# Four-chunk modulation tiles, a merged score product and alternating row halves in the first mixer of a diffusion backbone step

## The chip, the cores and the metric

The kernel runs on one core of one Trainium2 chip. The metric is the device time of one execution in microseconds. Before the change the median of three timed executions is 2934.5 us (2930.41 to 2939.74). One more execution was profiled; its own time is 2926.64 us and its span, from the first to the last instruction of the program, is 2924.9 us. All rows below come from that execution.

## The reference

One inference step for 128 context tokens and 1024 latent tokens, width 1024, in float32, through two layers. Each layer has a mixer and a SwiGLU channel mixer; both sit behind an RMSNorm that is shifted, scaled and gated by six vectors of a conditioning map. The change touches the conditioning map and the mixer of layer 0:

```python
sh1, sc1, g1, sh2, sc2, g2 = split(silu(c) @ w_ada[l] + b_ada[l], 6)      # for context and latent condition, both layers
h = rmsnorm(x, norm_mix) * (1 + sc1) + sh1
qa, ka, va, qb, kb, vb, rb, lr = split_cols(h @ w_in, SIZES_EVEN)
oa = windowed_attention(rope(qa), rope(ka), va, cached context keys, per-head sink)
# gated linear attention, per direction, in chunks of 64 tokens:
q_e, k_e, k_s = q*exp(bcum), k*exp(-bcum), k*exp(b_last - bcum)
o = where(mask, q_e @ k_e.T, 0) @ v + q_e @ S        # S: scanned state, S <- decay*S + k_s.T @ v
ob = rms(o_forward + flip(o_backward)) * gain * silu(rb)
x = x + g1 * (concat(oa, ob) @ w_out)
```

On the diagonal of a chunk the two decays cancel, so the forward and the backward score of a token with itself are both its plain q.k.

## The kernel before

Activations are kept transposed: 128 features on the partitions, 1152 tokens (128 context, 1024 latent) along the free dimension, in three chunks of 384 (`NCH`). Most products are made of three float32r matmuls over high and low parts (`mm3`, L147 to L149). The other matmuls are float32, and the profile shows two instructions for each of them. SBUF is handed out by hand as 34 slots (`us(i)`), two wider ones (`uc(0)`, `uc(1)`, shown as tile `c`), and small rings: `raw` (3 buffers of 128x1024, where weights land), `w` (4), `t` (5 of 128x384) and `ta` (3). PSUM has the rings `mm` (3 banks), `S` (2), `X` (2) and `O` (1).

The order of the instructions on each engine is set by the tile framework: it plans the program in a simulated time line (`schedule_with_timeline_sim`) and sorts independent work by that. Each engine then runs its list in order. Nearly all DMAs are issued by SyncE (SP), also in order, so a DMA that waits for its buffer holds back those behind it.

The stages of layer 0's mixer, in program order:

- Head. Four modulation units for the shift and scale of the first norm, the sum of squares of x, the first norm (`norm_k`, L268 to L274).
- Token-major and gate projections, `gla_pre`, then the projections of keys, values and queries. The change does not touch these.
- Nine turns of `attention(i - 1)`, each but the last followed by one projection (`proj`, L147 to L149) whose result is spilled to DRAM: i = 0 to 3 the queries and keys of the linear attention (`ev_spill`), i = 4 to 7 its gate `rb` with a SiLU (`ev_silu`, L984). An attention block computes scores per head (L771, L779), adds the mask and takes the maximum (L786), forms the negative bias (L789), the exponential with its sum (L791), transposes the probabilities (L803) and multiplies by the values (L814 to L816).
- Linear attention, four heads, in a software pipeline: `gla_a` (decays on DVE and ACT, products on POOL, L870, L880, L882; transposes L887; chunk states L902 with 64 contraction rows per direction, evicted by L913 on ACT and DVE), `gla_b` (four scans, L927 and L928, on DVE), `gla_c` (scores L947 with 64 contraction rows per direction, masked into two SBUF halves by a predicated copy L949, products with v L955 forward and L956 backward, product with the state L959), `gla_d` (RMS norm over the head, gain, and the product with the gate read back from DRAM, L975). Between them `out_a` multiplies the attention output with a quarter of the output projection.

A modulation unit (`ada_unit`) before covers 512 of the 6144 outputs of a layer. Its weights come as four DMAs of 512 KB (L188), each holding two contraction chunks of 128 for 512 columns. Each contraction chunk is one matmul (L192) with a stationary of 32 columns that writes a group of 32 PSUM partitions, group k % 4. ACT copies the 512 columns out (L195, twice 256), matmuls with a selector add the four groups (L198), DVE adds the bias (L203) and for scales the norm weight (L207). Four units run in the head, with slots of their own; twenty in the loop, through two buffers (`uc(0)`, `uc(1)`): two per turn at i = 5 to 8, then three after each `gla_c`.

Of the kernel before, what the change touches and what calls it, by code (L numbers as in the profile page):

```python
# [14 lines left out]
D = 1024  # L15
# [31 lines left out]
def body(tc, A):  # L47
# [6 lines left out]
    with contextlib.ExitStack() as ctx:  # L54
# [17 lines left out]
        mq = st.tile([128, 2, 128], U8, name="mq")  # L72
        dls = st.tile([128, 36], F32, name="dls")
# [106 lines left out]
        def ada_unit(l, u, raws=None, tag="mm"):  # L180
# [3 lines left out]
            for p in range(4):  # L184
                raw = raws[p] if raws else uc(aring[0] % 2)
                aring[0] += 1
                raw = raw[:, :D]
# [6 lines left out]
            for i in range(2):  # L194
                sc.copy(th[i], ps[:, i * 256:(i + 1) * 256])  # L195
            ps2 = ps[:, 0:8]
            for c in range(4):
                pe.matmul(ps2[:, 2 * c:2 * c + 2], th[c // 2][:, c % 2 * 128:(c % 2 + 1) * 128], sel[:, 0:2],  # L198
                          start=True, stop=True)
            j, k0 = u // 2, (u % 2) * 4  # L200
            m = mods[:, (l * 6 + j) * 16:(l * 6 + j + 1) * 16].rearrange("p (c k) -> p c k", c=2)[:, :, k0:k0 + 4]
            b = C_BADA + l * 48 + j * 8 + k0
            ve.tensor_tensor(out=m, in0=ps2.rearrange("p (k c) -> p c k", c=2),  # L203
                             in1=cols[:, None, b:b + 4].to_broadcast([128, 2, 4]), op=ALU.add)
            if j in (1, 4):
                n0 = (C_NMIX if j == 1 else C_NFFN) + l * 8 + k0
                ve.scalar_tensor_tensor(m, m, 1.0, cols[:, None, n0:n0 + 4].to_broadcast([128, 2, 4]),  # L207
                                        op0=ALU.add, op1=ALU.mult)
# [3 lines left out]
        def ada_all():  # L212
            for l in range(2):
                for u in range(12):
                    if l or u >= 4:
                        yield ada_unit(l, u)
# [355 lines left out]
        for u, s0 in ((0, 8), (2, 12)):  # L572
            ada_unit(0, u, [us(s0 + p) for p in range(4)], "X")
        rs = rstd_of(X, 0)
        etm_land(0)
        for u, ss in ((1, (4, 5, 6, 7)), (3, (28, 29, 30, 31))):
            ada_unit(0, u, [us(i) for i in ss], "X")
# [149 lines left out]
        def attention(b):  # L727
# [29 lines left out]
            for g in range(2):  # L757
# [3 lines left out]
                P = [PU[i // 2][:, (i % 2) * 512:(i % 2) * 512 + w] for i in range(4)]  # L761
                for i in range(4):
# [22 lines left out]
                    else:  # L785
# [3 lines left out]
                    ve.scalar_tensor_tensor(negm[:, i:i + 1], mx[:, i:i + 1], -0.125, nsink[:, h:h + 1],  # L789
                                            op0=ALU.mult, op1=ALU.min)  # L790
                    sc.activation(out=P[i], in_=src, func=AF.Exp, scale=0.125, bias=negm[:, i:i + 1],  # L791
                                  accum_out=ssum[:, i:i + 1])
# [32 lines left out]
        def ev_spill(dst, by):  # L825
            def ev(c, ps):
                t = tmp()
                if c != 1:
# [12 lines left out]
        def gla_init():  # L841
            mqf = tmpa(256)
            sy.dma_start(out=mqf, in_=A["gmask"])
            ve.tensor_copy(mq.rearrange("p a b -> p (a b)"), mqf)
# [4 lines left out]
        def gla_a(hd):  # L849
# [47 lines left out]
            for hf in range(2):  # L897
                p = slice(hf * 64, hf * 64 + 64)
                for b0, b1 in GRP:
                    ps = aux()  # L900
                    for b in range(b0, b1):
                        pe.matmul(ps[:, (b - b0) * 128:(b - b0 + 1) * 128], ktt[p, b * 128:(b + 1) * 128],  # L902
                                  vb3[p, b], start=True, stop=True)
                    pv = ps[:, :(b1 - b0) * 128].rearrange("p (b v) -> p b v", b=b1 - b0)
# [26 lines left out]
        def gla_c(hd):  # L931
# [6 lines left out]
            for b0, b1 in ((0, 4), (4, 8), (8, 9)):  # L938
                nb = b1 - b0
                t = G["AT"][atr[0] % 2]  # L940
                atr[0] += 1
                af, ab = t[:, 0:512], t[:, 512:1024]
                for q, at in ((0, af), (1, ab)):
                    ps = aux("X", 2)
                    p = slice(q * 64, q * 64 + 64)
                    for b in range(b0, b1):
                        pe.matmul(ps[:, (b - b0) * 128:(b - b0 + 1) * 128], kt[p, b * 128:(b + 1) * 128],  # L947
                                  qt[p, b * 128:(b + 1) * 128], start=True, stop=True)
                    ve.copy_predicated(at[:, :nb * 128].rearrange("p (b i) -> p b i", b=nb),  # L949
                                       mq[:, q:q + 1].to_broadcast([128, nb, 128]),  # L950
                                       ps[:, :nb * 128].rearrange("p (b i) -> p b i", b=nb))
# [28 lines left out]

        def ev_silu(dst):
            def ev(c, ps):
# [7 lines left out]
        for i in range(9):  # L990
# [3 lines left out]
            if i >= 5:  # L994
                ada_step(2)
# [417 lines left out]
```

## Time and profile before

| | |
|---|---|
| median of three timed executions | 2934.5 us |
| the profiled execution, its own time | 2926.64 us |
| its span | 2924.9 us |
| PE busy | 2747.6 us (94%) |
| DVE, ACT, POOL busy | 2096.2, 1318.0, 1299.6 us |
| mean granted TensorE clock | 0.962 of full speed |

A granted clock of 1.0 is TensorE's upper level of 2.4 GHz and 0.5 its lower one of 1.2 GHz; a mean in between is a stretch that held both. "Busy" for PE counts a matmul from its start to its modelled end, so that overlapping matmuls count once. An idle time is put down to the instruction that ended it. SP is the queue that issues DMAs. From 850 us on the kernel is the channel mixer of layer 0 and all of layer 1, whose code the diff leaves alone.

### The profile page before, as it was taken

What the parts mean: (1) busy time and instruction counts of PE and PEld (TensorE: products, weight loads), DVE (VectorE), ACT (ScalarE), POOL (GpSimd) and SP (SyncE); (2) the same over time, 40 slices, a digit from 0 to 9 for tenths busy, and PEclk for the clock granted to TensorE, in tenths of its full rate; (3) what the DMA queues carried; (4) which work ended last, traced back from release to release, by engine and by line L of the source; (5) the groups of instructions that cost most, each with busy time, mean ns of one, the idle gap of its engine ahead of it and who ended that gap; (6) DMA issues with size and microseconds to landing.
All of it is one profiled execution on the core that took longest, in us unless ns stands there. A gap on an engine that the chain in (4) does not pass through costs nothing. (4 is left out here: it accounts for less than half of the span.)

```text
span 2924.9 us, 47943 instructions
## 1 busy us (share of the span) xinstructions
PE 2747.6 (94%) x18456; PEld 2593.8 (89%) x18456; DVE 2096.2 (72%) x3589; ACT 1318.0 (45%) x2268; POOL 1299.6 (44%) x760
## 2 busy tenths in 40 slices
PE   6999989989999999999999999887899999999998
PEld 4889766766889999999999899787899999999998
DVE  5475667554388878777778787767688878778876
ACT  4344776322353433433534466544443444344333
POOL 4231013220365645555556533343555556355553
PEclk9999998799999999999999999999899999999999
DMA  7123357545253322632323223463253232533332
GB/s 274 57 82 100 105 157 231 152 143 166 72 212 95 98 87 82 214 102 85 92 89 105 72 83 114 130 212 130 100 184 93 89 94 86 188 91 114 95 89 69
DMA packets 138548, 353.55 MB, mean 121 GB/s; under 512 B 14768, under 2 KB 64304, under 8 KB 138320
## 3 DMA queue, kind: packets, MB, share of 16 engines
q1 hardware_dynamic: 136592, 343.42, 36.8%
q0 software_dynamic: 1728, 7.08, 0.7%
q8 instruction: 145, 2.38, 0.3%
q14 instruction: 83, 0.68, 0.1%
HBM read 286.14 MB, written 64.30 MB: 120 GB/s over the span
## 5 line engine op out<-in xcount | busy, mean ns | idle before, releaser
L147 PE MATMUL mm<-u,w 128*128 128x384 f32 (+1 forms) x1229 | 397.1, 324 | 10.7 <-DVE u L313 9.9
L148 PE MATMUL mm<-u,w 128*128 128x384 f32 (+1 forms) x1229 | 393.3, 320 | 3.8 <-POOL u L144 2.9
L149 PE MATMUL mm<-u,w 128*128 128x384 f32 (+1 forms) x1236 | 395.0, 320 | 0.0
L139 POOL TENSOR_TENSOR w<-raw,w 128x1024 fp32r<-128x1024 f32 (+2 forms) x67 | 148.3, 2214 | 384.1 <-ACT w L138 326.6
L147 PEld LDWEIGHTS mm<-u,w 128*128 128x128 f32 x1229 | 234.8, 191 | 30.8 <-issue 25.1
L149 PEld LDWEIGHTS mm<-u,w 128*128 128x128 f32 x1236 | 235.9, 191 | 8.1 <-issue 7.8
L148 PEld LDWEIGHTS mm<-u,w 128*128 128x128 f32 x1229 | 235.0, 191 | 5.7 <-POOL u L144 3.2
L149 PE MATMUL mm<-u,u 128*128 128x288 f32 x693 | 204.3, 297 | 0.4 <-POOL u L441 0.4
L147 PE MATMUL S<-u,w 128*128 128x288 f32 (+1 forms) x526 | 163.1, 311 | 39.9 <-ACT u L1158 17.8
L313 DVE SCALAR_TENSOR_TENSOR u<-mm,mods,u 128x288 f32<-128x288 f32 (+4 forms) x345 | 145.3, 452 | 69.7 <-PE mm L149 66.2
L147 PE MATMUL mm<-u,u 128*128 128x288 f32 x627 | 186.6, 298 | 3.7 <-ACT u L440 3.7
L148 PE MATMUL mm<-u,u 128*128 128x288 f32 x627 | 185.7, 296 | 0.0
L147 PE MATMUL X<-u,w 128*128 128x288 f32 (+1 forms) x571 | 174.3, 307 | 7.5 <-DVE u L144 2.4
L148 PE MATMUL X<-u,w 128*128 128x288 f32 (+1 forms) x571 | 175.1, 307 | 1.7 <-DVE u L274 1.7
L149 PE MATMUL X<-u,w 128*128 128x288 f32 (+1 forms) x573 | 175.0, 306 | 1.8 <-POOL w L139 1.2
L148 PE MATMUL S<-u,w 128*128 128x288 f32 (+1 forms) x526 | 161.5, 307 | 0.2 <-DVE u L144 0.2
L147 PE MATMUL mm<-u,c 128*128 128x288 f32 (+1 forms) x495 | 152.3, 308 | 2.4 <-DVE u L313 1.7
L149 PE MATMUL S<-u,w 128*128 128x288 f32 (+1 forms) x502 | 153.3, 305 | 0.0
L148 PE MATMUL mm<-u,c 128*128 128x288 f32 (+1 forms) x495 | 151.3, 306 | 0.0
L447 POOL TENSOR_TENSOR u<-raw 128x512 f32<-128x512 f32 x82 | 135.9, 1658 | 29.3 <-DMA raw<-in_w_fi_dram 13.7
L443 DVE TENSOR_TENSOR u<-u,raw 128x512 f32<-128x512 f32 x82 | 142.8, 1741 | 0.8
L147 PE MATMUL X<-u,u 128*128 128x288 f32 (+1 forms) x444 | 133.1, 300 | 7.0 <-DVE u L313 4.6
(430 smaller groups left out, 9327.6 us busy)
## 6 DMA issues: line engine op xcount, KB each, us to landing
raw<-in_w_fi_dram SPq DMA_DIRECT2D x164, 512.0 KB, 3.6
c<-in_w_ada_dram SPq DMA_DIRECT2D x80, 512.0 KB, 3.8
raw<-in_w_fo_dram SPq DMA_DIRECT2D x96, 384.0 KB, 3.1
d_w<-u SPq DMA_DIRECT2D x20, 512.0 KB, 3.4
u<-d_w SPq DMA_DIRECT2D x20, 512.0 KB, 5.4
u<-in_w_ada_dram SPq DMA_DIRECT2D x16, 512.0 KB, 10.3
raw<-in_w_fo_dram SPq DMA_DIRECT2D x16, 512.0 KB, 3.8
raw<-in_w_oi_dram SPq DMA_DIRECT2D x16, 512.0 KB, 4.0
```

Source lines behind the costliest of these rows:

```text
L139: gp.tensor_tensor(out=lo[:, :n], in0=raw[:, :n], in1=f_(hi[:, :n]), op=ALU.subtract)
L147: pe.matmul(ps, wh, hh, start=first, stop=False)
L148: pe.matmul(ps, wh, hl, start=False, stop=False)
L149: pe.matmul(ps, wl, hh, start=False, stop=last)
L313: ve.scalar_tensor_tensor(x, ps[:, s0:s1], mod(l, j, cond, n), x, op0=ALU.mult, op1=ALU.add)
L443: ve.tensor_tensor(out=s2, in0=s1, in1=a11, op=ALU.subtract)
L447: gp.tensor_tensor(out=s3, in0=a11, in1=a21, op=ALU.subtract)
```

## The change

- A modulation unit covers 256 outputs. One DMA of 512 KB now holds four contraction chunks for 256 columns, so that four matmuls for four different groups of 32 PSUM partitions follow each other. There are 24 units per layer with two DMAs each.
- The weights of the units in the loop land in five places in turn: the three buffers of the ring `raw`, which the weights of the projections use too, and `uc(0)` and `uc(1)`.
- Units are spread anew: two in each of the nine turns of the attention loop, six after each of the first three `gla_c`, the last four after the fourth. The head makes the same columns in the order shift, scale, shift, scale in steps of 256.
- In attention the bias is formed for two heads at once, after the scores of both, and then their two exponentials follow.
- The SiLU of the gate moves from the projection's eviction (now a plain DVE copy) to `gla_d`, where all three chunks are loaded first, into the ring `t`, then passed through the SiLU.
- In `gla_a` and `gla_c` the matmuls of the two row halves alternate, into two PSUM banks that are evicted afterwards.
- In `gla_c` both directions' scores are copied into one tile (the backward mask now leaves out the diagonal), POOL multiplies it by one plus the identity (`m2`), and one product with v replaces two.

```diff
@@ ada_unit
-            for p in range(4):
-                raw = raws[p] if raws else uc(aring[0] % 2)
+            for p in range(2):
+                if raws:
+                    raw = raws[p]
+                else:
+                    aring[0] = (aring[0] + 1) % 5
+                    raw = uc(aring[0] - 3) if aring[0] > 2 else pw.tile([128, D], F32, name="raw", bufs=3)
                 sy.dma_start(out=raw, in_=A["w_ada"][l, u, p])
-                for i in range(2):
-                    k = 2 * p + i
-                    g = k % 4
-                    pe.matmul(ps[32 * g:32 * g + 32, :], scp[:, k], raw[:, i * 512:(i + 1) * 512], start=k < 4, stop=k >= 4)
-            th = [tmp(256), tmp(256)]
+                for g in range(4):
+                    pe.matmul(ps[32 * g:32 * g + 32, :256], scp[:, 4 * p + g], raw[:, g * 256:(g + 1) * 256],
+                              start=p == 0, stop=p == 1)
+            th = tmp(256)
@@ attention
-                    ve.scalar_tensor_tensor(negm[:, i:i + 1], mx[:, i:i + 1], -0.125, nsink[:, h:h + 1],
+                    srcs.append(src)
+                    if i % 2 == 0:
+                        continue
+                    ve.scalar_tensor_tensor(negm[:, i - 1:i + 1], mx[:, i - 1:i + 1], -0.125, nsink[:, h - 1:h + 1],
                                             op0=ALU.mult, op1=ALU.min)
-                    sc.activation(out=P[i], in_=src, func=AF.Exp, scale=0.125, bias=negm[:, i:i + 1],
+                    for n in (i - 1, i):
+                        sc.activation(out=P[n], in_=srcs[n], func=AF.Exp, ...
@@ gla_a (the same alternation in gla_c)
-            for hf in range(2):
-                p = slice(hf * 64, hf * 64 + 64)
-                for b0, b1 in GRP:
-                    ps = aux()
-                    for b in range(b0, b1):
-                        pe.matmul(ps[:, (b - b0) * 128:(b - b0 + 1) * 128], ktt[p, b * 128:(b + 1) * 128],
+            for b0, b1 in GRP:
+                pp = [aux(), aux()]
+                for b in range(b0, b1):
+                    for hf in range(2):
+                        p = slice(hf * 64, hf * 64 + 64)
+                        pe.matmul(pp[hf][:, (b - b0) * 128:(b - b0 + 1) * 128], ktt[p, b * 128:(b + 1) * 128],
@@ gla_c
+                for q in range(2):
+                    ve.copy_predicated(at3, mq[:, q:q + 1].to_broadcast([128, nb, 128]), ...
+                gp.tensor_tensor(out=at3, in0=at3, in1=m2[:, None, :].to_broadcast([128, nb, 128]), op=ALU.mult)
-                    pe.matmul(po[:, o:o + 128], vb3[:, b], af[:, o:o + 128], start=True, stop=False)
-                    pe.matmul(po[:, o:o + 128], vb3[:, b], ab[:, o:o + 128], start=False, stop=False)
+                    pe.matmul(po[:, o:o + 128], vb3[:, b], at[:, o:o + 128], start=True, stop=False)
@@ gla_d
+            rts = [tmp() for c in range(NCH)]
+            for c in range(NCH):
+                sy.dma_start(out=rts[c], in_=d_r[hd][:, ch(c)])
+            for c in range(NCH):
+                sc.activation(out=rts[c], in_=rts[c], func=AF.Silu)
...
-                rt = tmpa()
-                sy.dma_start(out=rt, in_=d_r[hd][:, ch(c)])
-                ve.tensor_tensor(out=sd, in0=sd, in1=rt, op=ALU.mult)
+                ve.tensor_tensor(out=sd, in0=sd, in1=rts[c], op=ALU.mult)
@@ the loops
-            if i >= 5:
-                ada_step(2)
+            ada_step(2)
...
-        ada_step(3)
+        ada_step(6)
```

## Rows read from the trace of the kernel before

**Rows 1.** The page's first parts: busy time; granted clock in 40 slices.

```profile
PE 2747.6 (94%) x18456; PEld 2593.8 (89%) x18456; DVE 2096.2 (72%) x3589; ACT 1318.0 (45%) x2268; POOL 1299.6 (44%) x760
PEclk9999998799999999999999999999899999999999
```

**Rows 2.** Windows: length; PE, PEld, DVE, ACT, POOL busy (count); clock, DMA, GB/s.

```profile
0.00:50.00 50.00, 26.82 (x132) 12.98 (x133) 22.67 (x46) 21.00 (x47) 15.95 (x17) 0.90 0.89 327
230.00:425.00 195.00, 185.80 (x1111) 159.63 (x1109) 114.16 (x325) 129.59 (x267) 19.20 (x11) 0.98 0.36 111
425.00:490.00 65.00, 55.24 (x283) 36.84 (x285) 47.62 (x126) 44.77 (x102) 18.72 (x13) 0.89 0.77 222
490.00:757.00 267.00, 246.27 (x1329) 185.26 (x1326) 129.06 (x183) 80.84 (x148) 56.49 (x41) 0.85 0.52 160
516.00:552.00 36.00, 35.61 (x159) 28.37 (x159) 24.42 (x34) 13.50 (x28) 10.38 (x13) 0.51 0.51 146
604.00:624.00 20.00, 11.96 (x44) 6.47 (x43) 15.32 (x8) 3.38 (x4) 8.33 (x2) 0.66 0.35 116
725.00:757.00 32.00, 28.30 (x142) 19.09 (x142) 6.48 (x17) 4.71 (x11) 1.09 (x2) 0.89 0.51 166
```

**Rows 3.** Windows of line 192 alone, in the head.

```profile
18.43:19.50 1.07, 1.06 (x8) 0.16 (x8) 1.00 1.02 406
23.55:24.62 1.07, 1.05 (x4) 0.14 (x4) 1.00 1.06 421
```

**Rows 4.** Windows of line 192 alone: attention, then linear attention.

```profile
230.00:490.00 260.00, 29.86 (x122) 4.20 (x124) 0.96 0.46 139
490.00:757.00 267.00, 58.55 (x200) 7.20 (x196) 0.85 0.52 160
```

**Rows 5.** Waits, 490:757 on PE, 225:760 on SP: total, times, longest.

```profile
PE O L959 <- DVE u L928: 10.6, 2, 6.6
PE mm L192 <- DMA c<-in_w_ada_dram: 7.0, 5, 2.3
...
SPq L188 <- PE mm L192: 154.6, 62, 10.1
```

**Rows 6.** Windows of PE alone, mixed row halves, then one row half.

```profile
596.04:597.46 1.42, 1.42 (x19) 1.00 0.99 387
599.08:600.17 1.09, 1.09 (x9) 1.00 1.38 327
```

**Rows 7.** Lines 947 and 956: ns min/median/max, first and last start.

```profile
L947 PE MATMUL X<-u,u x144: 272/272/580, 491.3 to 671.4; 64*128 64x128 f32 x144
L956 PE MATMUL O<-u,u x72: 272/275/580, 502.7 to 717.7; 128*128 128x128 f32 x72
```

**Rows 8.** Line 913, the evictions of the chunk states.

```profile
L913 ACT COPY u<-S x20: 387/1108/1115, 484.5 to 668.8; 64x512 f32<-64x512 f32 x12, 64x128 f32<-64x128 f32 x4, 64x384 f32<-64x384 f32 x4
```

**Rows 9.** A POOL product (line 447), then scans beside POOL (timeline).

```profile
L447 POOL TENSOR_TENSOR u<-raw x82: 1277/1632/1826, 832.7 to 2849.4; 128x512 f32<-128x512 f32 x82
...
604.63 4.78 POOL L880 TENSOR_TENSOR u<-u,u 128x1152 f32<-128x1152 f32 x1 [5.05 <-DMA u<-d_qk]
607.00 4.82 DVE L928 TENSOR_TENSOR_SCAN u<-u,u 64x1152 f32<-64x1152 f32 x1
616.65 2.55 DVE L928 TENSOR_TENSOR_SCAN u<-u,u 64x1152 f32<-64x1152 f32 x1
```

**Rows 10.** Lines 984, 791, 831: table loads, a DVE eviction.

```profile
L984 ACT ACT_TABLE_LOAD  x12: 1283/1283/1283, 290.2 to 428.8; - x12
L791 ACT ACT_TABLE_LOAD  x11: 1283/1283/1283, 239.1 to 420.1; - x11
L831 DVE TENSOR_SCALAR t<-mm x4: 546/554/558, 223.7 to 276.8; 128x384 f32<-128x384 f32 x4
```

**Rows 11.** Weight loads: landing times of line 188, and line 139's split.

```profile
DMA to landing us min/median/max: 3.3/4.2/14.8
...
L139 POOL TENSOR_TENSOR w<-raw,w 128x1024 fp32r<-128x1024 f32 (+2 forms) x67 | 148.3, 2214 | 384.1 <-ACT w L138 326.6
```

More of the change, by code (lines that the diff above doesn't have):

```diff
@@ L72, in body @@
         mq = st.tile([128, 2, 128], U8, name="mq")
+        m2 = st.tile([128, 128], F32, name="m2")
         dls = st.tile([128, 36], F32, name="dls")
@@ L202, in ada_unit @@
+            th = tmp(256)
+            sc.copy(th, ps[:, :256])
+            ps2 = ps[:, 256:260]
+            for c in range(2):
+                pe.matmul(ps2[:, 2 * c:2 * c + 2], th[:, c * 128:(c + 1) * 128], sel[:, 0:2], start=True, stop=True)
+            j, k0 = u // 4, (u % 4) * 2
+            m = mods[:, (l * 6 + j) * 16:(l * 6 + j + 1) * 16].rearrange("p (c k) -> p c k", c=2)[:, :, k0:k0 + 2]
             b = C_BADA + l * 48 + j * 8 + k0
             ve.tensor_tensor(out=m, in0=ps2.rearrange("p (k c) -> p c k", c=2),
-                             in1=cols[:, None, b:b + 4].to_broadcast([128, 2, 4]), op=ALU.add)
+                             in1=cols[:, None, b:b + 2].to_broadcast([128, 2, 2]), op=ALU.add)
@@ L213, in ada_all @@
             for l in range(2):
-                for u in range(12):
-                    if l or u >= 4:
+                for u in range(24):
+                    if l or u >= 8:
                         yield ada_unit(l, u)
@@ L570, in etm_land @@
             sy.dma_start(out=land[q][:, :1088], in_=A["w_etm"][0, q])
-        for u, s0 in ((0, 8), (2, 12)):
-            ada_unit(0, u, [us(s0 + p) for p in range(4)], "X")
+        hraw = [us(i)[:, :D] for i in (8, 9, 10, 11, 12, 13, 14, 15)]
+        hraw += [us(i)[:, :D] for i in (4, 5, 6, 7, 28, 29, 30, 31)]
+        for n, u in enumerate((0, 4, 1, 5)):
+            ada_unit(0, u, hraw[2 * n:2 * n + 2], "X")
         rs = rstd_of(X, 0)
         etm_land(0)
-        for u, ss in ((1, (4, 5, 6, 7)), (3, (28, 29, 30, 31))):
-            ada_unit(0, u, [us(i) for i in ss], "X")
+        for n, u in enumerate((2, 6, 3, 7)):
+            ada_unit(0, u, hraw[8 + 2 * n:10 + 2 * n], "X")
         etm_land(1)
@@ L939, in gla_c @@
                 nb = b1 - b0
-                t = G["AT"][atr[0] % 2]
+                at = G["AT"][atr[0] % 2][:, :nb * 128]
                 atr[0] += 1
[L942 to L947, printed above, removed]
+                at3 = at.rearrange("p (b i) -> p b i", b=nb)
+                pp = [aux("X", 2), aux("X", 2)]
+                for b in range(b0, b1):
+                    for q in range(2):
+                        p = slice(q * 64, q * 64 + 64)
+                        pe.matmul(pp[q][:, (b - b0) * 128:(b - b0 + 1) * 128], kt[p, b * 128:(b + 1) * 128],
                                   qt[p, b * 128:(b + 1) * 128], start=True, stop=True)
-                    ve.copy_predicated(at[:, :nb * 128].rearrange("p (b i) -> p b i", b=nb),
-                                       mq[:, q:q + 1].to_broadcast([128, nb, 128]),
-                                       ps[:, :nb * 128].rearrange("p (b i) -> p b i", b=nb))
+                for q in range(2):
+                    ve.copy_predicated(at3, mq[:, q:q + 1].to_broadcast([128, nb, 128]),
+                                       pp[q][:, :nb * 128].rearrange("p (b i) -> p b i", b=nb))
+                gp.tensor_tensor(out=at3, in0=at3, in1=m2[:, None, :].to_broadcast([128, nb, 128]), op=ALU.mult)
                 po = aux("O", 1)
@@ L1028, in body @@
         gla_c(1)
-        ada_step(3)
+        ada_step(6)
         gla_b(2)
@@ L1381, in prep @@
     same = (ii // 64) == (jj // 64)
-    P["gmask"] = c_(np.concatenate([same & (ii <= jj), same & (ii >= jj)], axis=1).astype(f))
+    P["gmask"] = c_(np.concatenate([same & (ii <= jj), same & (ii > jj), 1 + (ii == jj)], axis=1).astype(f))
     return P
```

40 lines of the change are left out of this document (15 added, 25 removed).

## The prediction

> **What bounds the kernel now.** I read the page's shares first: PE is busy for 94% of the span and no other engine above 72% [rows 1]. A shorter piece on DVE, ACT or POOL is therefore worth something only where PE stands idle. The granted clock in 40 slices then shows one place ahead of the middle where it sags, slices 7 and 8, some 440 to 585 us [rows 1]; the change works there. The windows by stage are the view that decides. In the attention loop PE is busy for 185.8 of 195 us and then, when the projections run out, 55.2 of 65. In the linear attention it is busy for 246.3 of 267, at a mean clock of 0.85; from 516 to 552 it is busy throughout at 0.51, the lower level, and from 604 to 624 it is idle for 8 us at 0.66 [rows 2]. DVE has 129 of those 267 us, ACT 81, POOL 56. So between 230 and 757 us PE's own work sets the pace, with two gaps: waits for the scans, 10.6 us, and for modulation weights, 7.0 us [rows 5]. The stages that the diff doesn't name are taken as unchanged.
>
> **Modulation matmuls.** The head of the trace shows the packing that the change wants, by accident of what had landed: eight instructions (four matmuls, four groups of 32 columns) took 1.06 us, and four instructions (two groups) 1.05 [rows 3]. So twice the groups cost nothing, and a load of 512 KB, now four groups of 256 columns instead of two of 512, should take between half of 1.06 us and all of it. I take 0.60, factor 0.56: only the streaming halves, the start and drain stay. In the loop before, attention has 122 instructions, 30.5 loads, in 29.86 us, 0.98 each; the linear attention has 50 loads in 58.55 us, 1.17 each, as its clock is lower [rows 4]. After, 36 loads lie in attention and 44 behind it (18 and 22 units of two). Attention: 36 x 0.98 x 0.56 = 19.8, saving 10 us of PE. Linear attention: 44 x 1.17 x 0.56 = 28.8, saving 29.7. Bounds with factor 0.5 to 1: attention from a gain of 12 to a loss of 5, linear attention 33 to 7. Selector matmuls and ACT copies stay as many. There are twice the units, 20 more hand-overs PE to ACT to PE, which I put at nothing because other matmuls stand ready in PE's list; without that cover, 20 waits of 1.4 us (7.0 / 5, the load waits [rows 5]) are 28 us. DVE's additional bias additions are 128x4 and small.
>
> **Five places.** SP's modulation loads waited 154.6 us for PE to free one of two buffers, and everything behind them on SP waited too [rows 5]. Five places take most of that, and of PE's 7.0 us; I take 5. What is late next is the shared ring, the rival below.
>
> **Row halves.** Where the planner happened to run the two halves beside each other, 18 instructions took 1.42 us, 0.079 each; eight of one half took 1.09, 0.136 each (the windows count one neighbour's tail more) [rows 6]. Line 947 has 144 instructions [rows 7], line 902 by its loops as many. Full alternation saves 0.057 x 144 = 8.2 us in each. For 902 I count half: a four-block round is then 16 x 0.079 = 1.3 us, but its two banks need two ACT copies of 1.1 us [rows 8], and the round after the next can't start before. Less a sixth for what is paired already, 10 us, bounds 0 to 16. The Trainium skill says the same against this edit ("TensorEngine Tiling (Array Packing)", section "PSUM Bottleneck"): tiling speeds up TensorE, not the emptying of PSUM, which may become the limit. By that rule alone line 902 would give nothing and the 10 us would be some 7; the row of the copies agrees with it. Both banks now fill together, so a round can no longer overlap the copies of the one before: on eight four-block rounds 1.1 us each, 8.9 at most, during which all of PE's list stands behind it; I take 2, as PE has mostly been given other work there.
>
> **Merged product.** Line 956 goes: 72 instructions [rows 7] at 0.136 us [rows 6], 9.8 us of PE; at the packed spacing 5.7. In its place POOL multiplies eight tiles of 128x512, 1.63 us by the nearest row [rows 9], and four of 128x128 at a quarter: 14.7 us on an engine busy 56 of 267. The wait is new: PE's product with v stands behind DVE's two copies and POOL, and line 959 and whatever was sorted behind it stand behind that. All of it on the path is 14.7 us. POOL also slows DVE: a scan took 4.82 us beside a POOL product of 4.78 and 2.55 alone [rows 9], so 14.7 us of POOL can cost the scans 7 more. Between 0 and 22 I take 3, because the scores of the next head can be made during the wait and the masks of a head mostly don't meet scans.
>
> **SiLU and bias.** Twelve table loads for the SiLU and eleven back to the exponential, 1.28 us each [rows 10], leave the attention loop, 29.5 us of ACT, and 12 evictions of 0.55 us go to DVE. PE is idle there for only 19 us in all [rows 2]; I take 3 us, bounds 0 to 10. In `gla_d` at least 4 and at most 12 loads come back, 5 to 15 us on an ACT busy 81 of 267; hidden but at the last head, where out projections wait: 1 us. The paired bias halves 72 small DVE instructions and lets each first exponential wait for a second score. I put it at 0; the SiLU's bounds hold it.
>
> **Head.** Its 16 loads come in the same order, and DMA is the bound there (share 0.89, 327 GB/s [rows 2]), so PE's gain is hidden. The last unit now covers two of eight feature blocks instead of four, minus 1 us, between minus 3 and plus 2.
>
> **Sum.** Linear attention: PE work falls by 29.7 + 10 + 9.8 + 5 = 54.5 us of 246. Not all of it can show: DVE's four scans a head remain, and PE already waited 10.6 us for them. I count 60%, 33 us (bounds 30%, 16, to all, 54). Attention: 10 x 0.93 (PE's busy share of 230 to 490) + 3 = 12. Head 1. Costs 2 + 3 + 1 = 6. Together minus 40. The profiled execution took 2926.6 us, 7.9 below the median of the three runs, so 2886.6 for a run like it and 2894 for the median.
>
> **Rivals.** (a) *The chain through the scans takes over.* For it: the gap from 604 to 624, where DVE scans and PE waits. Against: 246 of 267 us busy. Then the linear attention gives at most 6 us for its costs of 6, attention 10: 2924. (b) *The clock gives it back.* From 516 to 552 us PE was busy for 35.6 of 36 us and yet at 0.51, nearly all of it the lower level [rows 2]. If freed time becomes idle time and two more stretches of 36 us run at that level, each costs 18 us: 2930; one of them, 2912. The Trainium skill ("TensorE: Matmul & The Clock Gate", part 1, section "HAM oscillation") says that gaps between matmul bursts send the clock back to its lower level; the gap from 604 to 624, PE busy for 12 of 20 us at 0.66, agrees. Against: packed groups and row pairs fill the array more. (c) *Slower: the shared ring `raw`.* Three of five modulation loads now sit between two weight loads, so a projection's weights can't be fetched before PE has eaten the modulation tile in front. A late fetch costs 4.2 us to land and 2.2 for POOL's split [rows 11], 6.4 in all, and eight projections and four quarters of the output projection are exposed: 77 us at most. It decides from eight late fetches of the twelve (51 us against the 40 gained): 2945 with eight, +11. Against: a turn of the loop is about 30 us long, time enough to fetch. (d) *All of it counts*, and the stretch at the lower level goes: linear attention 54, its half-clock stretch 18 of which I count 10, attention 15, costs 4: minus 75, 2860.
>
> **How the numbers follow.** Forecast 0.55 (its own range 2870 to 2912), (a) 0.17, (b) 0.08, (c) 0.10, (d) 0.10. The range from 2860 to 2926 leaves out (c), the worse half of (b) and half of (d), about 0.2. About 0.3%, 9 us, can be told from no change. Faster by more: the forecast, (d), half of (a) and of (b), 0.78. Within: the rest of (a) and (b), 0.12. Slower: (c), 0.10.
>
> **What would show it.** Right: line 192 with eight instructions in about 0.6 us and under 50 us of PE in all of the loop; lines 902 and 947 in pairs that start together; no table loads of the SiLU before the linear attention; the linear attention some 30 us shorter with PE idle longer in it. The forecast is wrong if PE waits in the projections for line 139 (ring), if the window of the linear attention keeps its length with more idle before line 959 (scans), or if the clock there falls under 0.85 (clock).

## The result, and the profile after

| | before | after |
|---|---|---|
| median of the runs beside each other | 2935.58 us (2930.41 to 2939.74, 4 runs) | 2896.32 us (2894.58 to 2902.01, 4 runs) |
| profiled execution, its span | 2926.64, 2924.9 us | 2896.55, 2894.7 us |
| end of attention to the start of the last output projection | 263.3 us | 236.6 us |

The ratio is 0.9872, 95% interval 0.9854 to 0.989: faster by 39 us. The two traces differ by 30.2 us only, since the profiled execution of before lay 9 us under its median; so they show three quarters of the gain. Lines of after stand a little lower in the code: the modulation matmul is L193, its load L191, scores L958, the copy of scores L961, POOL's mask L963, product with v L967, product with the state L970, the `mm3` products L148 to L150.

The page of after, busy time and granted clock, against [rows 1]: PE is busy for 23 us less, and the clock sags in slices 7 to 10, where before only slices 7 and 8 did.

```profile
PE 2724.6 (94%) x18768; PEld 2608.1 (90%) x18768; DVE 2102.1 (73%) x3598; ACT 1295.8 (45%) x2250; POOL 1293.9 (45%) x772
PEclk9999998788999999999999999999899999999999
```

To compare stages that shift, I cut both traces at the same instructions: first attention score, last product of attention with the values, last product with the state (L959 before, L970 after), first product of 288 columns, with which the last output projection begins. Windows of before, columns as in [rows 2]:

```profile
233.10:493.40 260.30, 242.62 (x1406) 197.01 (x1408) 164.06 (x456) 173.09 (x367) 39.13 (x24) 0.96 0.47 142
493.40:718.80 225.40, 208.37 (x1140) 160.73 (x1139) 118.77 (x156) 73.50 (x130) 51.85 (x37) 0.85 0.51 157
718.80:756.70 37.90, 34.20 (x168) 22.18 (x168) 7.16 (x18) 6.95 (x17) 3.13 (x2) 0.87 0.51 161
```

And of after:

```profile
241.00:486.50 245.50, 237.07 (x1602) 202.97 (x1603) 164.21 (x443) 135.58 (x332) 34.91 (x23) 0.98 0.51 167
486.50:704.70 218.20, 203.30 (x1230) 170.73 (x1232) 116.56 (x174) 85.14 (x146) 62.98 (x49) 0.76 0.48 153
704.70:723.10 18.40, 18.40 (x124) 17.28 (x125) 6.65 (x16) 10.91 (x19) 7.24 (x5) 0.96 0.57 190
```

Attention is 14.8 us shorter, the linear attention only 7.2, at a lower clock (0.76 for 0.85), and the stretch behind it 19.5. The head and the token-major products are 8 us longer, the part behind the mixer 3 to 4; the output projection itself is as long (48.3 us both times). The prediction's window of the linear attention held this last stretch too, but it had no term for how late the modulation's loads end. What fills the stretch, PE's lines show, of before and of after (busy, mean ns, idle before):

```profile
L192 PE MATMUL mm<-c,scp 128*32 128x512 f32 x40 | 13.1, 741 | 3.0 <-DMA c<-in_w_ada_dram 2.9
L148 PE MATMUL mm<-u,w 128*128 128x384 f32 x24 | 8.4, 350 | 0.0
```

```profile
L149 PE MATMUL mm<-u,w 128*128 128x384 f32 x24 | 8.0, 335 | 0.0
L193 PE MATMUL mm<-raw,scp 128*32 128x256 f32 x8 | 1.7, 572 | 0.0
```

Both hold the same 72 products of the last `out_a` quarter (24 on each of three lines). Before, ten late modulation loads (40 instructions) stand among them, 13.1 us, with their selectors and 3.0 us of waiting for their data. Why they are late, SP's timeline shows (start, length, line, tile, count), before and then after:

```profile
727.98 15.13 SPq L188 DMA_DIRECT2D c<-in_w_ada_dram  x5
743.20 16.04 SPq L1047 DMA_DIRECT2D t<-d_ob  x8
```

```profile
692.40 0.81 SPq L191 DMA_DIRECT2D c<-in_w_ada_dram  x2
693.30 0.38 SPq L191 DMA_DIRECT2D raw<-in_w_ada_dram  x1
```

Before, the last five loads go out over 15 us, one each time PE frees one of two buffers; with five places the last is out at 693.3 instead of 742.8. The loads that read the linear attention's output back (`d_ob`) stand behind them on SP, but by the profile that is not what decided: the first cast of these tiles waited for one of PE's last `out_a` products.

The modulation matmuls alone, in the three stretches, first before and then after (PE busy, count):

```profile
233.10:493.40 260.30, 30.59 (x126) 0.96 0.47 142
493.40:718.80 225.40, 44.70 (x158) 0.85 0.51 157
718.80:756.70 37.90, 13.11 (x40) 0.87 0.51 161
```

```profile
241.00:486.50 245.50, 25.64 (x288) 0.98 0.51 167
486.50:704.70 218.20, 33.08 (x310) 0.76 0.48 153
704.70:723.10 18.40, 1.67 (x14) 0.96 0.57 190
```

88.4 us became 60.4 (62.3 with 32 instructions that run ahead of the first attention score), and 40 late instructions at the end became 14. Waits of PE and SP, 225 to 760 us, against [rows 5]:

```profile
PE O L970 <- DVE u L939: 4.1, 1, 4.1
...
SPq L191 <- PE mm L193: 73.2, 36, 18.8
SPq L134 <- PE mm L193: 23.4, 7, 6.0
```

### The profile page after: what moved, and what is told of

It is laid out like the page before. It is cut to its first block, busy times and chain, and to the rows that moved or that the text cites. A ratio compares the mean times of both kernels' runs of the same rounds, so it can differ in the third digit from the quotient of the medians.

```text
span 2894.7 us, 48626 instructions
## 1 busy us (share of the span) xinstructions
PE 2724.6 (94%) x18768; PEld 2608.1 (90%) x18768; DVE 2102.1 (73%) x3598; ACT 1295.8 (45%) x2250; POOL 1293.9 (45%) x772
## 5 line engine op out<-in xcount | busy, mean ns | idle before, releaser
L148 PE MATMUL mm<-u,w 128*128 128x384 f32 (+1 forms) x1229 | 397.9, 324 | 13.3 <-DVE u L313 10.5
L150 PE MATMUL mm<-u,w 128*128 128x384 f32 (+1 forms) x1236 | 393.7, 320 | 0.0
L148 PEld LDWEIGHTS mm<-u,w 128*128 128x128 f32 x1229 | 236.1, 192 | 20.4 <-issue 14.8
L150 PEld LDWEIGHTS mm<-u,w 128*128 128x128 f32 x1236 | 235.7, 191 | 3.6 <-issue 3.4
L150 PE MATMUL mm<-u,u 128*128 128x288 f32 x693 | 203.9, 296 | 0.0
L148 PE MATMUL S<-u,w 128*128 128x288 f32 (+1 forms) x526 | 163.0, 311 | 40.1 <-ACT u L144 17.6
L148 PE MATMUL mm<-u,u 128*128 128x288 f32 x627 | 186.5, 298 | 4.6 <-ACT u L440 3.7
L148 PE MATMUL X<-u,w 128*128 128x288 f32 (+1 forms) x571 | 174.5, 307 | 7.7 <-DVE u L145 2.4
L150 PE MATMUL X<-u,w 128*128 128x288 f32 (+1 forms) x573 | 174.6, 305 | 1.0 <-DVE w L446 0.8
L150 PE MATMUL S<-u,w 128*128 128x288 f32 (+1 forms) x502 | 154.1, 307 | 0.0
L148 PE MATMUL mm<-u,c 128*128 128x288 f32 (+1 forms) x495 | 151.8, 307 | 2.4 <-DVE u L313 1.7
L148 PEld LDWEIGHTS S<-u,w 128*128 128x128 f32 x526 | 100.0, 191 | 44.7 <-ACT u L1164 18.7
```

The source lines that it names most:

```text
L148: pe.matmul(ps, wh, hh, start=first, stop=False)
L150: pe.matmul(ps, wl, hh, start=False, stop=last)
```

## The experiments

My theory after the comparison was still that of the prediction: less PE work, of which the packed modulation tile is the most. The rival: the landing places, which set when the modulation's loads go out and end. All kernels compute the whole reference. "Tail" is the time from the last product with the state to the end of the output projection, 86.2 us before and 66.7 after.

Each kernel was timed beside the kernel before, whose median there lay between 2930.4 and 2935.9 us. Differences in us between changed kernels are those of their medians; by the ratios they come out 1 to 3 us larger or smaller. Stages are read from one profiled execution of each kernel, which lay up to 11 us from that kernel's median.

**Undoing the tile's width.** Units of 512 columns as before, in five places, head as before:

```diff
-            for p in range(2):
-                for g in range(4): pe.matmul(ps[32 * g:32 * g + 32, :256], scp[:, 4 * p + g], ...)
+            for p in range(4):
+                for i in range(2): pe.matmul(ps[32 * g:32 * g + 32, :], scp[:, 2 * p + i], ...)   # g = (2 * p + i) % 4
```

> The changed kernel, but its modulation units are again 512 columns wide with two groups of 32 per load (and the head's units as before); five places, spread and all else stay. Theory (the packed matmuls are the largest part, PE's work is what shrinks): PE gets some 34 us of modulation work back in the loop, 60 to 90% of it shows: 20 to 30 us slower than the changed kernel, about 2916 to 2926. Rival (the gain came from the five places and the spread, the width is hidden): within 6 us of the changed kernel, 2890 to 2902.

Measured: 2891.54 us, ratio 0.9847 (0.9833 to 0.9862), no slower than the whole change. The theory fell. The modulation matmuls of this kernel, attention and linear attention, and then its timeline where loads had landed together:

```profile
233.70:480.70 247.00, 31.50 (x160) 0.98 0.53 171
480.70:697.90 217.20, 29.85 (x144) 0.79 0.46 148
```

```profile
574.85 0.62 PE L195 MATMUL mm<-c,scp 128*32 128x512 f32 x2
574.86 0.62 PE L195 MATMUL mm<-raw,scp 128*32 128x512 f32 x2
575.30 0.60 PE L195 MATMUL mm<-c,scp 128*32 128x512 f32 x2
575.31 1.46 PE L195 MATMUL mm<-raw,scp 128*32 128x512 f32 x10
576.59 1.03 PE L195 MATMUL mm<-c,scp 128*32 128x512 f32 x4
```

The timeline of before, same stage:

```profile
562.13 1.05 PE L192 MATMUL mm<-c,scp 128*32 128x512 f32 x4
566.10 1.05 PE L192 MATMUL mm<-c,scp 128*32 128x512 f32 x4
```

Before, one load (4 instructions, two groups) runs alone for 1.05 us. With five places five loads, 20 instructions, follow each other in 2.77 us, 0.55 each: consecutive loads write different groups, so the packing comes about by itself. 31.50 + 29.85 = 61.35 us against 60.4 with the narrow tile. Width and places buy much the same PE time: 65.4 us with the width and two places, 70.9 with the places alone, in the same windows of the next two kernels.

**Undoing the places.** Two landing places instead of five:

```diff
-                    aring[0] = (aring[0] + 1) % 5
-                    raw = uc(aring[0] - 3) if aring[0] > 2 else pw.tile([128, D], F32, name="raw", bufs=3)
+                    aring[0] = (aring[0] + 1) % 2
+                    raw = uc(aring[0])
```

> The changed kernel with the modulation loads of the loop in two places again (the two wide slots), all else as changed. By the run with 512-column units the width is worth nothing in the loop, so the gain of 15 us in attention and of 20 us between the last state product and the feed-forward must have another cause. Theory A (the places: SyncE no longer stands behind PE's modulation matmuls): 12 us or more slower, 2908 to 2925, with the long stretch after the last state product back at about 86 us. Rival B (spread or SiLU): within 5 us of 2896.

Measured: 2931.76 us, 0.9983 (0.9968 to 0.9998): almost all of the gain is gone, more than the theory's 2925. Attention takes 255.5 us (after: 245.5), the linear attention 234.2 (218.2), the tail 77.0 (66.7); so the late end of the loads has only 10 us of the loss, and 16 lie in the linear attention, at a clock of 0.70. Its wait on SP, its last load, its linear attention:

```profile
SPq L191 <- PE mm L193: 138.7, 57, 11.3
...
L191 SPq DMA_DIRECT2D c<-in_w_ada_dram x80: 327/328/1734, 41.1 to 740.9; - x80
```

```profile
497.00:731.20 234.20, 210.38 (x1249) 170.83 (x1248) 118.08 (x174) 86.62 (x148) 65.64 (x49) 0.70 0.48 151
```

The last modulation load is at 740.9 again, though this kernel's modulation matmuls took only 65.4 us of PE by the same windows. All else of the change, PE time saved included, bought 4 us without the places.

**The places alone**, put into the kernel before:

```diff
-                raw = raws[p] if raws else uc(aring[0] % 2)
-                aring[0] += 1
+                ... five places as in the change
```

> The kernel before with the five places alone. Theory (SyncE standing behind two buffers is what cost attention's end and the end of the linear attention): attention 8 us or more shorter and the stretch after the last state product 10 us or more shorter: 2905 to 2918. Rival (the places only serve the change's own spread and order): within 6 us of 2935.

Measured: 2920.31 us, 0.9957 (0.9942 to 0.9972): 13 us of the 39, a little short of the theory; the tail is 12.6 us shorter, attention 4.6, not the 8 expected. The last load goes out at 716.0.

**Undoing the spread.** Units only in the last four turns of the attention loop:

```diff
-            ada_step(2)
+            if i >= 5:
+                ada_step(4)
```

> The changed kernel with the loop's early modulation units in the last four turns of attention again (four in each turn, then six, six, six and six). Theory (where the units stand matters little as long as five places hold their loads): within 5 us of 2896. Rival (the spread lets attention's last turns, which wait on DVE and ACT, run free): attention 8 us or more longer, 2904 to 2912.

Measured: 2909.16 us, 0.9908 (0.9888 to 0.9928), 13 slower than the change. That is the rival's time but not its reason: attention is 3 us shorter, and the loss lies in the linear attention, at a clock of 0.70:

```profile
483.20:717.00 233.80, 219.17 (x1239) 179.08 (x1238) 118.60 (x175) 86.40 (x148) 61.46 (x47) 0.70 0.47 146
```

**Undoing the alternation, the merged product.** Halves one after the other; two masked halves and two products without POOL:

```diff
-                for b in range(b0, b1):
-                    for hf in range(2):
+            for hf in range(2):
+                for b0, b1 in GRP:
```

> The changed kernel, but the two row halves are not alternated in either place, each half's matmuls stand together as before. Theory: 10 us of PE come back, 60% shows: 4 to 8 us slower, 2900 to 2904. Rival (the planner pairs halves by itself, and filling both banks together costs as much as pairing gives): within 3 us, or a little faster.

```diff
-                gp.tensor_tensor(out=at3, in0=at3, in1=m2[...], op=ALU.mult)
-                    pe.matmul(po[:, o:o + 128], vb3[:, b], at[:, o:o + 128], start=True, stop=False)
+                    pe.matmul(po[:, o:o + 128], vb3[:, b], af[:, o:o + 128], start=True, stop=False)
+                    pe.matmul(po[:, o:o + 128], vb3[:, b], ab[:, o:o + 128], start=False, stop=False)
```

> The changed kernel, but the scores of the two directions stay in two tiles with two products with v and without POOL's product. Theory: PE gets 10 us back, less 3 us for POOL's wait: 2 to 6 us slower, 2898 to 2902. Rival (POOL's product, its wait and what it does to the scans cost as much as the second product): 0 to 6 us faster, 2890 to 2896.

Measured: 2910.79 us, 0.9913 (0.9897 to 0.9929) without alternation; 2921.05, 0.9951 (0.9939 to 0.9964) without the merge, both slower than either of their expectations. The linear attention of the first and of the second:

```profile
486.10:712.60 226.50, 199.40 (x1226) 170.99 (x1227) 123.66 (x172) 84.76 (x144) 70.05 (x48) 0.76 0.45 148
```

```profile
488.60:723.30 234.70, 215.07 (x1300) 182.33 (x1302) 112.59 (x173) 87.81 (x148) 50.20 (x37) 0.76 0.45 142
```

With the merge PE is busy 11.8 us less at the same clock (215.1 to 203.3; 9.8 was forecast), and it idles 4.7 us less (19.6 to 14.9). The alternation saves no busy PE time at all (199.4 without it, 203.3 with it, same clock); its 8 us in this stage are idle time, 27.1 to 14.9. (That profiled execution without alternation took 2899.47 us, 11 under its kernel's median, so it shows only 3 us of the loss.)

The reason that no PE time is saved stands in PE's list after the change:

```profile
575.83 1.16 PE L912 MATMUL S<-u,u 64*128 64x128 f32 x16
...
582.33 1.16 PE L912 MATMUL S<-u,u 64*128 64x128 f32 x8
583.83 1.16 PE L912 MATMUL S<-u,u 64*128 64x128 f32 x8
```

An alternated round, 16 instructions, takes the 1.16 us that 8 instructions of one half take. But few rounds are alternated: the planner mostly put the halves apart again. Of the 288 instructions of L912 and L958, 32 start within 0.07 us of the one ahead of them; before the change it was 39 (L902 and L947), and it would be 144 with full alternation. So what undoing this edit costs is not the pairing. By the profile, the longest of the waits that came with it ended with the bias addition of a modulation unit, as waits of the control further down do (9.2 us):

```profile
PE X L957 <- DVE mods L203: 9.1, 1, 9.1
```

**Undoing the SiLU's move.**

```diff
-            ... ev_spill(d_r[i - 4], None)
+            ... ev_silu(d_r[i - 4])
```

> The changed kernel with the SiLU back in the projection's eviction and the gate loaded chunk by chunk in the linear attention. Theory (the table loads were hidden behind a busy PE): within 5 us, attention at most 4 us longer, 2894 to 2902. Rival (attention was paced by ACT and the chain through it): attention 10 to 15 us longer, 2905 to 2912.

Measured: 2914.79 us, 0.9925 (0.9906 to 0.9944), 18 slower, which neither expectation holds. Not where the table loads are: attention takes 245.8 us with them and 245.5 without. The linear attention takes 231.1, at 0.73:

```profile
488.20:719.30 231.10, 208.37 (x1229) 173.04 (x1233) 120.42 (x176) 77.07 (x134) 66.19 (x50) 0.73 0.47 149
```

**Nothing undone**, a control: the turn of the five places starts two places later, no instruction more or less.

```diff
-        aring = [0]
+        aring = [2]
```

> The changed kernel with one thing shifted that does no work: the turn of the five places starts at another place, so the planner sorts part of the program anew. Theory: the parts decide, a new sorting moves the time by at most 4 us: 2892 to 2900. Rival (how the planner sorts is worth as much as the smaller parts): 6 us or more either way, and then no part under 6 us can be told by undoing it.

Measured: 2901.88 us, 0.9895 (0.9881 to 0.9909), 5.6 us above the change, with intervals that overlap a little; the linear attention takes 228.9 us instead of 218.2. So the planner's order alone is worth some 5 us in the end and 10 in this stage. A kernel described under "The head" says more: only the order of four and four units of the head differs, and it is 9 us slower, with this linear attention:

```profile
488.00:719.90 231.90, 215.38 (x1248) 176.84 (x1246) 114.08 (x175) 90.37 (x151) 64.66 (x49) 0.72 0.45 145
```

That is 13.7 us longer, in an execution 6 us above its median, with no edit in the stage. Undone edits of 5 to 15 us, and sums of them, have to be read with that: the alternation (14), the spread (13) and the SiLU (18) are not clearly beyond it, the merge (25) and the places (35) are.

The stage's length goes with its clock, roughly. In the seven kernels that keep all edits on PE's work, the linear attention takes 218.2 us at a mean clock of 0.76 (the change), 216.6 at 0.74 (the last kernel below), 228.9 at 0.75, 231.1 at 0.73, 231.9 at 0.72, and 234.2 and 233.8 at 0.70. That is a relation over single traces; what brings the clock down isn't shown.

**Undoing all that saves PE work**, width, alternation and merge together; places, spread, SiLU and bias stay:

```diff
-            for p in range(2):                       # modulation unit: 256 columns, four groups a load
+            for p in range(4):                       # 512 columns, two groups a load
...
-                for b in range(b0, b1):
-                    for hf in range(2):
+            for hf in range(2):
+                for b0, b1 in GRP:
...
-                gp.tensor_tensor(out=at3, in0=at3, in1=m2[...], op=ALU.mult)
```

> The changed kernel without the three edits that take work off PE: 512-column units, row halves one after the other, two products with v and no product on POOL. Five places, spread, SiLU and paired bias stay. Theory (places and spread make the gain, PE's saved work is given back by the clock): 2898 to 2908, most of the gain kept. Rival (the parts add up as the single runs read: halves 14, merged product 25, width minus 5): 2925 to 2935, no gain left.

Measured: 2907.01 us, 0.9918 (0.9901 to 0.9935). About 24 us of gain remain, three fifths of the change's 39; the three together are worth 11 to 14, while undone one by one they gave -5, 14 and 25. Against the kernel with wide units alone (2891.54), alternation and merge together are worth 15 by medians, 21 by ratios.

**The clock.** Wide units, and the dense first quarter of the output projection moved ahead of the first scans, into the stretch at the lower clock:

```diff
+        out_a(0)
         gla_b(0)
...
-        out_a(0)
         gla_a(2)
```

> The version with 512-column units and otherwise all of the change (2891.5), with one call moved: the first quarter of the output projection stands before the first head's states instead of behind its norm, so that its dense products lie in the stretch from about 485 to 540 us that ran at the lower clock. No work is added or left out. Theory (in the linear attention the time saved on PE is given back by the clock, which stays low while PE runs only short products): the long stretch at the lower level, 48 us in that version, shrinks to half or less, and the linear attention gets 10 to 20 us shorter: 2872 to 2882. Rival (the scans and evictions pace that stretch whatever the clock): within 4 us of 2891, with PE idle longer there.

Measured: 2900.73 us, 0.9889 (0.9872 to 0.9906), some 10 us slower than the same kernel without the move (2891.54, 0.9847). Its linear attention, and behind it that of the kernel without the move:

```profile
486.90:710.70 223.80, 203.65 (x1090) 155.54 (x1090) 120.58 (x160) 82.30 (x145) 64.28 (x47) 0.82 0.48 158
```

```profile
480.70:697.90 217.20, 196.02 (x1065) 161.58 (x1065) 117.86 (x166) 84.12 (x146) 67.81 (x48) 0.79 0.46 148
```

The clock rose from 0.79 to 0.82 (the longest stretch at the lower level shrank from 48 to 17 us, as the theory wanted) and the stage still grew by 6.6 us; neither expected time was met. But the stage isn't the same work: 176 modulation instructions lie in it where 144 did, eight loads that attention had. Over attention, linear attention and tail the kernel takes 10.1 us more, and 7.5 of them are additional idle time of PE. So this run doesn't tell what the clock is worth.

**The head.** The token-major stage takes 77.6 us before and 84.6 after. First the order of the eight narrow units put back (shift, shift, scale, scale):

```diff
-        for n, u in enumerate((0, 4, 1, 5)):
+        for n, u in enumerate((0, 1, 4, 5)):
```

> The changed kernel with the head's eight units in the order of columns as before (shift, shift, scale, scale). The trace shows 7 us more in the token-major products than before, and the run with 512-column units has none of that. Theory (the order shift, scale makes the planner put the norms of the second and third chunk late): 5 to 8 us faster, 2888 to 2891. Rival (it is the narrower units' more and smaller steps on DVE, whatever their order): within 3 us.

Measured: 2905.3 us, 0.9898 (0.9879 to 0.9917); the stage still takes 84.0. The order is not it. Then the changed kernel with four wide units in the head alone:

```diff
-        for n, u in enumerate((0, 4, 1, 5)):
-            ada_unit(0, u, hraw[2 * n:2 * n + 2], "X")
+        for u, s0 in ((0, 8), (2, 12)):
+            ada_head(0, u, [us(s0 + p) for p in range(4)], "X")     # 512 columns
```

> The changed kernel with the head's four modulation units as before (512 columns, two groups, order shift, scale, shift, scale in halves, their weights from a second array in the old layout); the loop keeps its narrow units. Theory (the narrower units of the head cost the token-major stage 7 us: all kernels with wide head units have it at 77.6 to 78.4 us, all with narrow ones at 83.7 to 86.7): that stage back under 79 us, the whole kernel some 7 us under the changed one, 2886 to 2892. Rival 1 (the 7 us come from the loop's units or the array's layout, not from the head): the stage stays at 83 to 87 us, time 2894 to 2900. Rival 2 (the stage is shorter, but the planner sorts the later stages anew, worth some 5 us either way, and the clock with it): stage under 79 us, time 2893 to 2902.

Measured: 2893.94 us, 0.9859 (0.9838 to 0.9881). The stage is back at 77.6 us, so it is the narrow units. Where the time goes, the products of L612 show, in the changed kernel and then, as L638, in this one (PE busy, count):

```profile
37.80:58.20 20.40, 9.23 (x28) 0.83 0.68 225
58.20:82.50 24.30, 10.86 (x35) 0.93 0.27 89
```

```profile
36.60:58.20 21.60, 9.62 (x28) 0.76 0.69 233
58.20:75.90 17.70, 10.14 (x35) 1.00 0.38 126
```

Up to 58.2 us both are equally far; the next 35 products take 24.3 us with narrow units and 17.7 with wide ones. In the changed kernel PE waits there for the last addition of the sum of squares for the second chunk's norm, which DVE ends at 62.9 us, and at 57.9 with wide units:

```profile
PE S L230 <- DVE t L255: 3.1, 1, 3.1
```

So the narrow units make this norm late; by what way isn't traced. Only 2.4 of the 7 us reach the end, within the overlap of the two intervals: the tail is 5.0 us longer (71.7). Of all kernels run, the change with wide units everywhere (2891.54) and this one are the fastest.

## Why the prediction was right, and where it was not

The total was right, 2896 for 2894, and so were the windows it was summed over: attention 14.8 us shorter for 12, linear attention with what follows up to the last output projection 26.7 for 27 (33 less the costs of 6). Against that, 11 us were lost in the head and behind the mixer, where a gain of 1 was forecast; so the two traces, of which that of before lay 9 us under its median, differ by 30 us and not by 40. The reasons were right in part only, and the total owes something to luck.

- **Modulation matmuls.** A load takes what I said: eight instructions in 0.64 us for 0.60 (timeline of after, below). PE's time for them in the three stretches is 60.4 us where I had 48.6, so 28 are saved for 39.7: the factor 0.56 was taken of 0.98 us, 0.55 a load, where one by itself takes 0.64, and part of them ran at the lower level (16 instructions in 1.93 us at 597.9). The step that failed is that the tile's width brings it: in the loop before, loads ran alone because they came one at a time, and the places cure that as well. [rows 3] had shown it: its four matmuls of four groups are two loads of the kernel before, which ran side by side without any wider packing in the code. The width is worth nothing in time (2891.54 without it).

```profile
573.99 0.64 PE L193 MATMUL mm<-c,scp 128*32 128x256 f32 x8
574.44 1.46 PE L193 MATMUL mm<-raw,scp 128*32 128x256 f32 x18
```

- **Five places, priced at 5 us.** This is the term that was mis-sized most: alone 13 us, undone in the whole change 35, of which the tail has 10, attention 10 and the linear attention 16. I read the right row, SP's 154.6 us [rows 5], and then priced only the 7 us that PE showed as waiting. But a stream held back by two buffers ends late, and its last ten loads stood in PE's list ahead of the last products that the output projection needs. Over the kernels, the tail follows how far the last modulation matmul ends behind the last product with the state: 30.6 us, tail 86.2 (before); 19.0, 77.0 (two places); 5.5, 73.6 (places alone); 5.0, 69.2 (spread undone); 4.0, 71.7 (wide units in the head alone); under 2.2 in the others with five places, 63 to 67. This accounts for the tail alone; why attention and the linear attention are shorter with five places isn't shown.
- **Rival (c), the shared ring.** Measured: the projections' loads waited for the modulation 23.4 us on SP, and PE's waits for a weight split stayed under 2 us. So the ring did not decide.
- **Merged product.** PE's 9.8 us are there by the traces (11.8), though another kernel that keeps the merge shows 215.4 us of busy PE in this stage, at a clock of 0.72, so the size isn't sure. The wait for POOL is not: PE waits once for L963, 0.4 us, and its large products took 1.27 us for the 1.63 reckoned. In time it is worth more than its PE work, 25 us undone; the excess isn't explained.

```profile
L963 POOL TENSOR_TENSOR u<-u,m x12: 451/1266/1285, 499.0 to 692.7; 128x512 f32<-128x512 f32 x8, 128x128 f32<-128x128 f32 x4
```

- **Row halves.** The step that failed is "full alternation": the code alternates, PE's list mostly doesn't, since the planner sorts independent matmuls anew. 32 instructions of 288 stand in pairs, 39 before, so the 10 us of [rows 6] can't be there, and PE's busy time didn't fall. An alternated round does cost what I reckoned or less (1.16 us for 1.3). The 14 us that undoing it costs in time lie near what a new sorting alone costs. The sentence of the Trainium skill that I weighed here ("TensorEngine Tiling (Array Packing)", section "PSUM Bottleneck") would have given 3 us less PE work; with hardly any round packed, these traces don't test it.
- **SiLU and bias.** The table loads went about as counted: 24 of 27 left attention, and behind it there are 15 for 9, four of them for the SiLU. Attention gained nothing from it (245.8 to 245.5), as its 19 us of idle time warned. The loss when it is undone lies in the linear attention (13 us) and is not explained; a kernel whose places only start elsewhere and one with another order in the head moved that stage by 11 and 14. The bias alone was not tried.

```profile
L982 ACT ACT_TABLE_LOAD  x4: 1283/1283/1283, 555.8 to 709.7; - x4
```

- **Head.** Minus 1 predicted, plus 7 measured in its stage, because with narrow units the second chunk's norm comes 5 us later and PE stands for it; I had looked at PE's and the DMAs' time there and not at DVE's chain, and the bound of plus 2 was too tight.
- **Sum, and rivals (a) and (b).** Over the window of the 54.5 us PE's busy time fell by 21 (208.4 + 34.2 to 203.3 + 18.4), 16 of them in the last stretch; in the linear attention proper it fell by 5 and the stage by 7. Rival (b) came true there in its size: at 0.85 of 225.4 us 34 were lost to the clock, at 0.76 of 218.2 us 52, the 18 that one more stretch was priced at. As an estimate, if all that ran at the lower level had taken half the time at the upper one, the stage would have gone from 191 to 166 us: 25 saved, of which the clock took 18 back. It was outweighed by the tail, for which I had no term, and by attention. My argument against (b), that packed groups and row pairs fill the array more, isn't borne out: the row pairs never came about, and with the packed groups the clock fell all the same. The rule of the Trainium skill beside it ("TensorE: Matmul & The Clock Gate", section "HAM oscillation", gaps send the clock back) accounts for it in part: PE idled for 4.0 us just ahead of the fall at 484 us, and for 5.1 us around the one at 658. But the clock also fell with PE busy throughout:

```profile
573.00:587.00 14.00, 14.00 (x121) 10.63 (x120) 9.11 (x16) 9.29 (x16) 1.73 (x2) 0.99 0.79 260
587.00:599.00 12.00, 12.00 (x65) 8.07 (x69) 6.49 (x8) 2.67 (x5) 3.56 (x5) 0.50 0.41 126
```

What brings it down there stays open. Rival (a) isn't borne out: PE's waits for the scans fell from 10.6 to 4.1 us.

- **The signs I had named.** The narrow load in about 0.6 us and the SiLU's table loads behind attention came true. Under 50 us of modulation matmuls (62.3), row pairs that start together, and a linear attention some 30 us shorter with PE idle longer (7.2 us, idle 14.9 for 17.0) did not; and one sign of being wrong did: the clock under 0.85.

So the range held, and that the forecast's size fits is luck in good part, errors that cancel: PE work that I counted at 60%, of which the row pairs never came about and the lower clock took much of the rest back, a head that got slower, and a stream of loads that I counted at PE's own wait and that was worth several times that.

## What to carry to other kernels

A stream of loads that waits for its buffers is to be priced by where it ends, not by the wait that the compute engine shows: look for its last load, and for the work that stands behind that load's matmuls in the engine's list. Before changing a tile so that matmuls pack, see whether they would pack by themselves if their data landed together; after it, see whether the order that the code asks for stands in the engine's list at all. And run a control that changes only the planner's order, before believing single undone edits of a few us.

## What was not expected of the hardware

Two-group loads of 512 columns that have landed together ran at 0.55 us each, where one alone takes 1.05: matmuls of different loads that write different groups of 32 columns overlap by themselves. Two 64-row halves whose matmuls alternate run in the time of one: 16 instructions in 1.16 us, as 8 of one half. And the linear attention, whose PE busy and idle time both fell (208.4 to 203.3 and 17.0 to 14.9 us), ran at a mean granted clock of 0.76 instead of 0.85; at 587 us the clock went to its lower level with PE busy for all of the 14 us ahead of it.
